# First two input blocks take the mLSTM keys' weights along; tokens held in quarter-feature tiles

## The chip, the cores and the metric

The kernel runs on one core of a Trainium2 chip. The metric is the time of one execution on that core in microseconds (us), taken as the median of several runs. The engines named below are TensorE (PE, with its weight loads as PEld), VectorE (DVE), ScalarE (ACT), GpSimd (POOL) and SyncE (SP), which here does little but issue DMAs.

## What is computed

Two transformer blocks in a row on 256 tokens of 2048 features, in float32. Only the beginning of the first one is touched. There, an input `x` (256 tokens) and a context `ctx` (256 tokens) are normalised, scaled and shifted by a modulation that is itself computed from `w_mod`, and multiplied with one wide weight matrix `w_in`:

```
mod   = c_act  @ w_mod + b_mod          # for x;   mod_c = cc_act @ w_mod + b_mod  for ctx
h     = rmsnorm(x,   g_norm1) * (1 + sc1)  + sh1
hc    = rmsnorm(ctx, g_norm1) * (1 + csc1) + csh1
z     = h @ w_in        # and hc @ w_in
gq, gk, gv, gg, glr, mq, mk, mv, mo, mgate = split(z)   # columns: gk at 512, gv at 1024,
                                                        # mq at 3088, mk (mLSTM keys) at 3600, mv at 4112
ml_k  = mk.reshape(heads) * DK ** -0.5
```

Everything after it (the gated linear attention and mLSTM scans, the output projection `w_out`, the feed-forward network, and the whole second block) is left as it is.

## The kernel before

Float32 operands are split in two: `split_w` lets ACT cast a raw weight unit to a high part `wh` (L187), and DVE subtract to get the low part `wl` (L188). A product then takes three matmuls (`mm3`, L208 to L210: high by high, high by low, low by high). A weight unit is 512 KB, 256 rows of 512 columns, one DMA by SP (`load_raw`, L172), and `units` gives them one after the other. The pools of `raw`, `wh` and `wl` have 4 buffers each. The pool `b8` has 14 buffers of 8 KB per partition; it holds the tokens, the transposed activations `hc` and `hl` (two parts each), the accumulators `gvc` and `gv`, and also the tiles `wm` of modulation weights that SP loads (L475). PSUM has four `acc` banks, three `ps` banks and one `mod` bank.

The inputs stage (`mix_in`) runs over 8 blocks of 256 features. For block b, `pieces(b)` multiplies the block's slice of `hl` and `hc` (four token tiles, `forms`) with three weight units: the GLA keys (columns 512 to 1023, summed over all blocks in the four `acc` banks), and the GLA values in two halves, whose part sums DVE adds into `gvc` and `gv` (L612 and L614). One piece is one token tile by one unit: 6 matmuls of 512 columns. Then come the 8 matmuls of the gates (L630). Between the pieces the next block is made ready: `mod_pe` for block b+1 in five steps, of which four load one `wm` tile (512 KB in two DMAs, L475) and multiply it (L481) and the last one evacuates the sum (ACT L486, PE transposes L488, DVE L490, L497, L499); and `hidden(b+1, 0)` and `hidden(b+1, 1)`, which transpose the tokens of x and of ctx (L305), scale and shift them (DVE L314, ACT L312) and split them (ACT L290, DVE L291). A block can't start on PE before that.

After the eight blocks comes the keys stage: `a_form` multiplies all 16 feature tiles with the mLSTM keys' weights (column 3600) in 8 units of 24 matmuls, and `k_evac` copies the four sums out of PSUM on ACT (L678) and transposes two of them (L684). Queries and values stages follow.

Two streams of side work hang on the main loops. Each unit that `units` yields calls `tick()`, which advances the stream `mods` (the remaining modulation vectors, `mod_vec`: each step loads one 512-KB tile of `w_mod`, L172, and DVE folds it in with two operations, L514 and L516) and the stream `side`. `mods` is set up at block 4 and runs at a rate of one step per unit there and in the keys stage. In `mix_out`, when the output projection has been written down, L1197 forces the steps that are still missing (`while self.mods_done < 12`).

The program is written in this order, and a scheduler then sets each engine's order by priority and by when operands are there; the two casts of a weight unit have a raised priority. In each engine the instructions run in that order.

The tokens are in four `b8` tiles, two halves of the features for x (`xt[2]`, `xt[3]`) and for ctx (`xt[0]`, `xt[1]`). A half is free again after the last of its four blocks has been transposed.

## Time and profile before

| | |
|---|---|
| median of 3 runs | 2670.62 us (2667.31 to 2674.35) |
| the profiled execution | 2672.57 us |
| its span in the trace | 2670.4 us |
| granted clock, mean | 0.991 of full speed |
| PE busy | 2603.5 us, 97% of the span |
| DVE busy | 1846.4 us, 69% |
| ACT busy | 1281.8 us, 48% |
| HBM read and written | 556.4 MB, 208 GB/s over the span |

2.2 us of the profiled execution lie outside its span. The times of the rows below count from the span's start. The inputs stage ends and the keys stage begins at some 240 us, the queries follow at some 300 us, and the forced steps of the modulation lie at 712 to 726 us.

### The profile page before, as it was taken

To read this page: it belongs to the slowest core of one execution; us is meant where nothing else is said; L and a number is where in the kernel's file an instruction comes from. 1 tells how busy PE (TensorE), PEld (TensorE's weight loads), DVE (VectorE), ACT (ScalarE), POOL (GpSimd) and SP (SyncE) were. 2 spreads that over 40 slices of the span, in tenths; PEclk is the share of its full clock that TensorE was granted. 3 is DMA by queue.
4 is the path that set the end of the run, shared out by engine and by line. 5 is a ranking of instruction groups with operands and counts; after the bars stand their busy time and mean duration, and the time that the engine had idled before them with its cause. 6 is when DMAs were issued, how large, how long until landed. Compare 5 with 4: busy or idle time off the path is not lost.

```text
span 2670.4 us, 37499 instructions
## 1 busy us (share of the span) xinstructions
PE 2603.5 (97%) x14093; PEld 2190.4 (82%) x14093; DVE 1846.4 (69%) x3006; ACT 1281.8 (48%) x2008; POOL 26.5 (1%) x52
## 2 busy tenths in 40 slices
PE   5999999999899999999999999999999999999999
PEld 3666888877778888888888988888888889998888
DVE  4466678787778988857856867677755566666665
ACT  2223323344365555544534554555544455657553
POOL 1000000000000000000000000000000000000000
PEclk8999999999999999999999999999999999999999
DMA  9775466678876666666675666556665567645664
GB/s 333 246 239 173 143 211 199 226 224 265 274 260 220 210 220 206 226 218 205 204 243 179 215 190 189 190 189 189 197 232 189 185 208 215 166 143 173 201 217 159
DMA packets 345271, 558.89 MB, mean 209 GB/s; under 512 B 30692, under 2 KB 129178, under 8 KB 342402
## 3 DMA queue, kind: packets, MB, share of 16 engines
q1 hardware_dynamic: 339800, 548.54, 63.9%
q10 hardware_dynamic: 4746, 7.11, 0.7%
q8 instruction: 110, 1.80, 0.3%
q0 software_dynamic: 544, 0.86, 0.1%
q14 instruction: 71, 0.58, 0.1%
HBM read 541.75 MB, written 14.69 MB: 208 GB/s over the span
## 4 chain that ended last, share of the span: by engine, by line
PE 82%; DMA 8%; DVE 6%; ACT 2%; issue 2%; SPq 1%; POOL 0%; ACTq 0%; DVEq 0%
PE acc L237 20%; PE acc L210 10%; PE acc L208 10%; PE acc L209 10%; PE acc L238 10%; PE mod L237 5%; DMA raw<-in_w_in_dram 3%; PE mod L238 2%; PE mod L209 2%; PE mod L210 2%; PE mod L208 2%; DMA raw<-in_w_mod_dram 2%; DVE wl L188 2%; DMA raw<-in_w_out_dram 1%; DVE ev L516 1%
## 5 line engine op out<-in xcount | busy, mean ns | idle before, releaser
L188 DVE TENSOR_TENSOR wl<-raw,wh 128x1024 fp32r<-128x1024 f32 (+4 forms) x804 | 965.7, 1205 | 578.2 <-ACT wh L187 575.5
L187 ACT CAST wh<-raw 128x1024 fp32r<-128x1024 f32 (+4 forms) x804 | 829.6, 1036 | 1068.0 <-PE acc L210 345.7
L237 PE MATMUL acc<-b,wh 128*128 128x512 f32 x2336 | 821.1, 394 | 0.0
L238 PE MATMUL acc<-b,wl 128*128 128x256 f32 x2336 | 634.4, 281 | 1.1 <-DVE wl L188 1.0
L208 PE MATMUL acc<-wh,b 128*128 128x512 f32 (+3 forms) x1580 | 585.3, 373 | 10.0 <-ACT b L290 7.6
L209 PE MATMUL acc<-wl,b 128*128 128x512 f32 (+3 forms) x1580 | 586.6, 371 | 7.5 <-DVE wl L188 7.3
L210 PE MATMUL acc<-wh,b 128*128 128x512 f32 (+3 forms) x1580 | 576.2, 370 | 1.1 <-DVE b L291 0.6
L237 PEld LDWEIGHTS acc<-b,wh 128*128 128x128 f32 x2336 | 434.1, 188 | 88.9 <-issue 0.7
L238 PEld LDWEIGHTS acc<-b,wl 128*128 128x128 f32 x2336 | 438.9, 188 | 15.0 <-DVE wl L188 2.4
L208 PEld LDWEIGHTS acc<-wh,b 128*128 128x128 f32 x1580 | 298.8, 189 | 71.8 <-ACT b L290 9.4
L209 PEld LDWEIGHTS acc<-wl,b 128*128 128x128 f32 x1580 | 299.2, 189 | 62.1 <-DVE wl L188 12.6
L210 PEld LDWEIGHTS acc<-wh,b 128*128 128x128 f32 x1580 | 297.0, 189 | 55.6 <-DVE b L319 4.0
L516 DVE SCALAR_TENSOR_TENSOR ev<-raw,cs,ev 128x512 f32<-128x512 f32 x240 | 179.4, 747 | 59.1 <-DMA raw<-in_w_mod_dram 56.4
L237 PE MATMUL mod<-b,wh 128*128 128x512 f32 x576 | 215.5, 396 | 0.6 <-DVE t L249 0.6
L238 PE MATMUL mod<-b,wl 128*128 128x256 f32 x576 | 161.5, 280 | 0.7 <-DVE wl L188 0.7
L237 PEld LDWEIGHTS mod<-b,wh 128*128 128x128 f32 x576 | 108.4, 188 | 23.5 <-DVE t L249 1.1
L1367 DVE SCALAR_TENSOR_TENSOR t<-t,convw,t 128x189 f32<-128x189 f32 (+2 forms) x344 | 126.9, 423 | 0.0
L238 PEld LDWEIGHTS mod<-b,wl 128*128 128x128 f32 x576 | 108.3, 188 | 3.9 <-DVE wl L188 1.1
L208 PE MATMUL mod<-wh,b 128*128 128x512 f32 (+2 forms) x274 | 96.9, 354 | 0.0
L209 PE MATMUL mod<-wl,b 128*128 128x512 f32 (+2 forms) x274 | 96.7, 353 | 0.0
L210 PE MATMUL mod<-wh,b 128*128 128x512 f32 (+2 forms) x274 | 96.5, 352 | 0.0
L290 ACT CAST b<-t 128x256 fp32r<-128x256 f32 x123 | 47.2, 405 | 64.2 <-DVE t L314 44.1
(357 smaller groups left out, 2469.0 us busy)
## 6 DMA issues: line engine op xcount, KB each, us to landing
raw<-in_w_up_dram SPq DMA_DIRECT2D x160, 512.0 KB, 4.5
raw<-in_w_mod_dram SPq DMA_DIRECT2D x128, 512.0 KB, 4.5
raw<-in_pool_w_in_dram SPq DMA_DIRECT2D x128, 512.0 KB, 3.8
raw<-in_w_in_dram SPq DMA_DIRECT2D x96, 512.0 KB, 4.9
raw<-in_w_down_dram SPq DMA_DIRECT2D x83, 512.0 KB, 4.8
b<-in_w_mod_dram SPq DMA_DIRECT2D x64, 512.0 KB, 7.9
raw<-in_pool_w_out_dram SPq DMA_DIRECT2D x64, 512.0 KB, 4.0
raw<-in_ple_w_gate_dram SPq DMA_DIRECT2D x64, 512.0 KB, 3.9
```

Source lines behind the costliest of these rows:

```text
L187: nc.scalar.copy(wh[:, :n], raw[:, :n])
L188: nc.vector.tensor_tensor(out=wl[:, :n], in0=raw[:, :n], in1=wh[:, :n].bitcast(F32), op=ALU.subtract)
L208: mm(out, lh, rh, start=first, stop=False)
L209: mm(out, lh, rl, start=False, stop=False)
L210: mm(out, ll, rh, start=False, stop=last)
L237: mm(acc, wh[:, i, o], f.both(kt), start=kt == k_first, stop=False)
L238: mm(acc[:, :T], wl[:, i, o], f(kt)[0], start=False, stop=kt == k_last)
L290: nc.scalar.copy(h, src)
L516: nc.vector.scalar_tensor_tensor(out=ev, in0=rv[:, i, :], scalar=cc, in1=ev, op0=ALU.mult, op1=ALU.add)
L1367: nc.vector.scalar_tensor_tensor(out=ov[:, r0:r1, c0:c1], in0=uv[:, r0 + dy:r1 + dy, c0 + dx:c1 + dx], scalar=tap(ky, kx), in1=ov[:, r0:r1 ...
```

## The change

The tokens go into four tiles that x and ctx share: tile q holds the features 512q to 512q+511 of both, and so belongs to the blocks 2q and 2q+1. Each input is loaded in four DMAs of 512 KB instead of two of 1 MB, and scaled by 8 DVE operations of 512 columns instead of 4 of 1024.

The blocks 0 and 1 (`early = 2`) load the mLSTM keys' weights of their rows as a fourth unit, multiply them in four more pieces each, and DVE puts the sums into a new `b8` tile `mk0`. The keys stage then runs over the remaining 6 units, and `k_evac` adds `mk0` on DVE while it evacuates, and scales on ACT afterwards.

```diff
     def tokens(self, i, src):
-        for half in range(2):
-            self.xt[i + half] = self.b8((P, 2, 1024))
-            self.nc.sync.dma_start(self.xt[i + half], src[0, :, half * 1024:(half + 1) * 1024].rearrange(
+        for q in range(4):
+            if self.xt[q] is None:
+                self.xt[q] = self.b8((P, 4, 512))
+            self.nc.sync.dma_start(self.xt[q][:, i:i + 2, :], src[0, :, q * 512:(q + 1) * 512].rearrange(
                 "(t p) n -> p t n", p=P))
...
-                for half, tt in ((0, 0), (0, 1), (1, 0), (1, 1)):
-                    t = self.xt[i + half][:, tt, :]
+                for q, tt in [(q, tt) for q in range(4) for tt in range(2)]:
+                    t = self.xt[q][:, i + tt, :]
                     nc.vector.tensor_scalar(out=t, in0=t, scalar1=r[:, tt:tt + 1], scalar2=None, op0=ALU.mult)
...
+        early = 2
+        mk0 = self.b8((P, 4, 512))
...
+            if b < early:
+                for tt in order:
+                    acc = self.ps()
+                    self.a_form([acc], [forms[tt]], ws[b, 3], kts[0], kts[-1])
+                    add(mk0[:, tt, :], acc)
+                    yield 1
...
-                ws[b, i] = list(self.units(w, 512 + 512 * i, 512, range(*blocks[b])))
+                ws[b, i] = list(self.units(w, 512 + 512 * i if i < 3 else 3600, 512, range(*blocks[b])))
...
         weights(0, 2)
+        weights(0, 3)
...
                     weights(b + 1, 2)
+                    if b + 1 < early:
+                        weights(b + 1, 3)
...
-                nc.scalar.activation(out=t, in_=accs[tt], func=AF.Copy, scale=scale)
+                if part is None:
+                    nc.scalar.activation(out=t, in_=accs[tt], func=AF.Copy, scale=scale)
+                else:
+                    nc.vector.tensor_tensor(out=t, in0=accs[tt], in1=part[:, tt, :], op=ALU.add)
+                    nc.scalar.mul(t, t, scale)
...
-        self.a_form(accs, forms, self.units(w, 3600, 512, range(16)), 0, 15)
-        self.mkc = k_evac(accs, self.mk, float(P) ** -0.5)
+        self.a_form(accs, forms, self.units(w, 3600, 512, range(2 * early, 16)), 2 * early, 15)
+        self.mkc = k_evac(accs, self.mk, float(P) ** -0.5, mk0)
```

PE at the end of block 0, before. The last piece of the values ends, then come the fourth `wm` tile of block 1's modulation (L481), the gates (L630), the transposes that evacuate the modulation (L488) and the first tile of block 2's modulation; `acc` with `wh_59` opens block 1.

```order
L209 MATMUL ps_87_424<-wl_57_257,b8_11_120 128x512
L210 MATMUL ps_87_424<-wh_56_256,b8_11_120 128x512
L481 MATMUL mod_61_272<-b8_71_342,cs_81 32x512 x4
L630 MATMUL ps_88_432<-b8_11_120,t4_53_246 112x256 x4
L630 MATMUL ps_88_432<-b8_15_124,t4_53_246 112x256 x4
L488 MATMUL mod_61_272<-cst_68,t2_72_349 128x128 x4
L481 MATMUL mod_92_454<-b8_93_455,cs_81 32x512 x4
L208 MATMUL acc_22_131<-wh_59_262,b8_15_124 128x512
L209 MATMUL acc_22_131<-wl_60_263,b8_15_124 128x512
L208 MATMUL acc_23_132<-wh_59_262,b8_15_124 128x512
L209 MATMUL acc_23_132<-wl_60_263,b8_15_124 128x512
```

The same place on PE in the changed kernel, from the end of the first added piece (`ps_95`); the fourth `wm` tile stands six matmuls ahead of these rows (lines of the file have moved by one here).

```order
L208 MATMUL ps_95_457<-wh_60_275,b8_17_132 128x512
L209 MATMUL ps_95_457<-wl_61_276,b8_17_132 128x512
L210 MATMUL ps_95_457<-wh_60_275,b8_17_132 128x512
L489 MATMUL mod_65_291<-cst_68,t2_76_368 128x128 x4
L208 MATMUL ps_96_465<-wh_60_275,b8_17_132 128x512
L209 MATMUL ps_96_465<-wl_61_276,b8_17_132 128x512
L210 MATMUL ps_96_465<-wh_60_275,b8_17_132 128x512
L208 MATMUL ps_96_465<-wh_60_275,b8_17_132 128x512
L209 MATMUL ps_96_465<-wl_61_276,b8_17_132 128x512
L210 MATMUL ps_96_465<-wh_60_275,b8_17_132 128x512
L208 MATMUL acc_24_139<-wh_63_281,b8_17_132 128x512
L209 MATMUL acc_24_139<-wl_64_282,b8_17_132 128x512
```

Between the modulation's last multiply and block 1 stand two of block 0's four added pieces, while the gates and block 2's first modulation tile have moved behind the opening of block 1.

DVE at the same place, before: the copies of block 0's last pieces (L612), the reduction of the modulation (L490), its vectors (L497, L499), and the scale and shift of block 1's tokens (L314), with the low parts of two weight units (L188) in between.

```order
L612 COPY b8_24_133<-ps_87_424 128x512
L612 COPY t2_19_128<-ps_88_432 112x512
L490 TENSOR_REDUCE sm_73_355<-mod_61_272 128x8
L188 TENSOR_TENSOR wl_78_379<-raw_76_376,wh_77_378 128x1024
L497 TENSOR_TENSOR mod0_97<-sm_73_355,vec1_87 128x4
L497 TENSOR_TENSOR mod1_98<-sm_73_355,vec1_87 128x4
L188 TENSOR_TENSOR wl_91_445<-raw_89_442,wh_90_444 128x1024
L499 TENSOR_TENSOR mod1_98<-mod1_98,vec1_87 128x4
L314 TENSOR_SCALAR t1_80_387<-ps_79_382,mod1_98,mod0_97 128x256
L314 TENSOR_SCALAR t1_85_416<-ps_84_411,mod1_98,mod0_97 128x256
L291 TENSOR_TENSOR b8_15_124<-t1_80_387,b8_15_124 128x256
```

DVE there in the changed kernel: L616 copies a piece, L491, L498 and L500 are the modulation, L314 the tokens.

```order
L616 COPY b8_27_142<-ps_94_449 128x512
L188 TENSOR_TENSOR wl_82_398<-raw_80_395,wh_81_397 128x1024
L616 COPY b8_26_141<-ps_95_457 128x512
L491 TENSOR_REDUCE sm_77_374<-mod_65_291 128x8
L498 TENSOR_TENSOR mod0_101<-sm_77_374,vec1_91 128x4
L498 TENSOR_TENSOR mod1_102<-sm_77_374,vec1_91 128x4
L500 TENSOR_TENSOR mod1_102<-mod1_102,vec1_91 128x4
L314 TENSOR_SCALAR t1_87_412<-ps_86_407,mod1_102,mod0_101 128x256
L314 TENSOR_SCALAR t1_92_441<-ps_91_436,mod1_102,mod0_101 128x256
L616 COPY b8_26_141<-ps_96_465 128x512
L291 TENSOR_TENSOR b8_17_132<-t1_87_412,b8_17_132 128x256
```

The weight units no longer stand between the modulation and L314; a copy of the added pieces stands ahead of the modulation, and one behind L314.

DVE at the first block's context tokens, before: `t1_46` is the transposed context, L447 casts the masks, L291 makes the low part.

```order
L188 TENSOR_TENSOR wl_57_257<-raw_55_254,wh_56_256 128x1024
L188 TENSOR_TENSOR wl_60_263<-raw_58_260,wh_59_262 128x1024
L291 TENSOR_TENSOR t4_53_246<-t4_52_239,t4_53_246 128x8x48
L291 TENSOR_TENSOR t4_54_247<-t4_52_239,t4_54_247 128x8x48
L314 TENSOR_SCALAR t1_46_222<-ps_45_217,mod1_98,mod0_97 128x256
L447 CAST lev_988<-t4_182_989 128x896
L291 TENSOR_TENSOR b8_11_120<-t1_46_222,b8_11_120 128x256
```

In the changed kernel L314 stands ahead of the second L188 and the L291 of this low part ahead of the masks' cast (L448):

```order
L188 TENSOR_TENSOR wl_58_270<-raw_56_267,wh_57_269 128x1024
L314 TENSOR_SCALAR t1_47_235<-ps_46_230,mod1_102,mod0_101 128x256
L188 TENSOR_TENSOR wl_61_276<-raw_59_273,wh_60_275 128x1024
L291 TENSOR_TENSOR t4_54_259<-t4_53_252,t4_54_259 128x8x48
L291 TENSOR_TENSOR t4_55_260<-t4_53_252,t4_55_260 128x8x48
L291 TENSOR_TENSOR b8_13_128<-t1_47_235,b8_13_128 128x256
L616 COPY b8_28_143<-ps_68_324 128x512
L616 COPY b8_28_143<-ps_73_345 128x512
L448 CAST lev_1077<-t4_197_1078 128x896
L291 TENSOR_TENSOR b8_13_128<-t1_48_239,b8_13_128 128x256
```

What moved there is the masks' cast, from one place ahead of the L291 to three places behind it.

SP at the end of the output projection (`w_out`), before: five units of `w_mod` after the last unit of `w_out`, of those that L1197 forces.

```order
L172 DMA raw_1005_5548<-in_w_mod_dram 128x2x512
L172 DMA raw_1006_5552<-in_w_out_dram 128x4x256
L172 DMA raw_1011_5593<-in_w_mod_dram 128x2x512
L172 DMA raw_1012_5597<-in_w_mod_dram 128x2x512
L1183 DMA t2_992_5450<-gtd_1024 128x256
L172 DMA raw_1013_5601<-in_w_mod_dram 128x2x512
L172 DMA raw_1014_5605<-in_w_mod_dram 128x2x512
L172 DMA raw_1015_5609<-in_w_mod_dram 128x2x512
L172 DMA raw_1018_5621<-in_w_mod_dram 128x2x512
```

SP there in the changed kernel:

```order
L172 DMA raw_1012_5573<-in_w_mod_dram 128x2x512
L172 DMA raw_1013_5577<-in_w_out_dram 128x4x256
L172 DMA raw_1018_5618<-in_w_mod_dram 128x2x512
L172 DMA raw_1019_5622<-in_w_mod_dram 128x2x512
L1200 DMA t2_997_5467<-gtd_1113 128x256
L172 DMA raw_1020_5626<-in_w_mod_dram 128x2x512
L172 DMA raw_1021_5630<-in_w_mod_dram 128x2x512
L172 DMA raw_1022_5634<-in_w_mod_dram 128x2x512
L172 DMA raw_1023_5638<-in_w_mod_dram 128x2x512
L172 DMA raw_1024_5642<-in_w_mod_dram 128x2x512
L172 DMA raw_1027_5654<-in_w_mod_dram 128x2x512
```

Two more units of `w_mod` come after the last one of `w_out`, seven in place of five.

## Rows read from the trace of the kernel before

**Rows 1.** The page's first part: the span, and busy time of each engine.

```profile
span 2670.4 us, 37499 instructions
PE 2603.5 (97%) x14093; PEld 2190.4 (82%) x14093; DVE 1846.4 (69%) x3006; ACT 1281.8 (48%) x2008; POOL 26.5 (1%) x52
```

**Rows 2.** Stretches: engines' busy us (instructions), PEclk granted clock, DMA share, GB/s.

```profile
40.00:60.00 20.00, 17.07 (x84) 10.98 (x88) 8.96 (x16) 2.32 (x4) 2.52 (x5) 0.91 1.09 361
60.00:80.00 20.00, 17.12 (x81) 10.64 (x73) 7.46 (x16) 5.75 (x10) 0.00 (x0) 0.83 0.73 249
200.00:220.00 20.00, 16.94 (x85) 11.09 (x84) 14.64 (x29) 5.14 (x9) 0.00 (x0) 1.00 0.91 291
260.00:280.00 20.00, 20.00 (x77) 14.13 (x76) 11.09 (x20) 9.38 (x12) 0.00 (x0) 1.00 0.26 79
```

**Rows 3.** PE's timeline, block 0 to 1: start, duration, instruction, [idle before <- releaser].

```profile
35.91 0.30 PE L305 MATMUL ps<-cst,b 128*128 128x128 f32 x1 [1.22 <-issue]
...
42.36 0.79 PE L208 MATMUL acc<-wh,b 128*128 128x512 f32 x1 [3.02 <-ACT b L290]
...
45.85 0.73 PE L210 MATMUL acc<-wh,b 128*128 128x512 f32 x2 [0.57 <-DVE b L291]
...
54.17 0.40 PE L209 MATMUL ps<-wl,b 128*128 128x512 f32 x1
...
56.49 0.40 PE L210 MATMUL ps<-wh,b 128*128 128x512 f32 x1
...
62.85 1.06 PE L481 MATMUL mod<-b,cs 128*32 128x512 f32 x8 [0.44 <-DVE sm L490]
66.35 0.80 PE L208 MATMUL acc<-wh,b 128*128 128x512 f32 x1 [2.44 <-ACT b L290]
66.94 0.63 PE L209 MATMUL acc<-wl,b 128*128 128x512 f32 x1
...
69.50 0.63 PE L209 MATMUL ps<-wl,b 128*128 128x512 f32 x1
...
71.64 0.63 PE L208 MATMUL acc<-wh,b 128*128 128x512 f32 x1
```

**Rows 4.** DVE's timeline at the same place.

```profile
59.89 0.69 DVE L612 COPY b<-ps 128x512 f32<-128x512 f32 x1 [2.28 <-PE ps L210]
...
62.71 1.22 DVE L188 TENSOR_TENSOR wl<-raw,wh 128x1024 fp32r<-128x1024 f32 x1
...
63.99 1.22 DVE L188 TENSOR_TENSOR wl<-raw,wh 128x1024 fp32r<-128x1024 f32 x1
...
65.32 1.00 DVE L314 TENSOR_SCALAR t<-ps,mod,mod 128x256 f32<-128x256 f32 x2
```

**Rows 5.** PE's timeline: modulation multiplies in block 4 (first two rows) and block 6.

```profile
144.83 1.07 PE L481 MATMUL mod<-b,cs 128*32 128x512 f32 x8
...
149.20 1.06 PE L481 MATMUL mod<-b,cs 128*32 128x512 f32 x8
...
201.29 1.06 PE L481 MATMUL mod<-b,cs 128*32 128x512 f32 x8 [0.30 <-DMA b<-in_w_mod_dram]
```

**Rows 6.** SP's timeline: DMA issues around the same two places.

```profile
129.79 4.85 SPq L475 DMA_DIRECT2D b<-in_w_mod_dram  x4
...
180.35 0.38 SPq L172 DMA_DIRECT2D raw<-in_w_in_dram  x1
195.82 2.02 SPq L475 DMA_DIRECT2D b<-in_w_mod_dram  x4
```

**Rows 7.** DVE's timeline in the forced steps of the modulation.

```profile
720.05 1.54 DVE L516 SCALAR_TENSOR_TENSOR ev<-raw,cs,ev 128x512 f32<-128x512 f32 x2 [0.36 <-DMA raw<-in_w_mod_dram]
722.13 1.54 DVE L516 SCALAR_TENSOR_TENSOR ev<-raw,cs,ev 128x512 f32<-128x512 f32 x2 [0.55 <-DMA raw<-in_w_mod_dram]
```

**Rows 8.** PE's timeline at the end of the forced steps.

```profile
725.81 1.84 PE L543 MATMUL ps<-cst,ev 128*128 128x2 f32 x8 [4.41 <-DVE ev L516]
```

**Rows 9.** Waits, 232 to 320 us: total, times, longest us.

```profile
ACT t L678 <- PE acc L210: 2.3, 3, 0.8
```

**Rows 10.** The page's DMA issues: times, KB each, median us to landing.

```profile
b<-in_w_mod_dram SPq DMA_DIRECT2D x64, 512.0 KB, 7.9
```

8 lines of the change are left out of this document (4 added, 4 removed).

## The prediction, made before the changed kernel was run

> **What bounds the kernel now.** I read the page's totals first: PE is busy for 97% of the span, DVE for 69% [rows 1]. So time is to be had only where PE stands still or where its clock is low, and moving work from a full stage into a hole is worth just what the hole holds. The table of stretches shows where holes are: in 40 to 80 us PE has about 17 busy us of 20, at a granted clock of 0.91 and 0.83, and in 260 to 280 us, the keys stage, it has all 20 at 1.00 [rows 2]. Next I read PE's timeline through the first hole, for the idle times in brackets and their releasers. Between block 0 and block 1 it waits 0.44 us for DVE's reduction and 2.44 us for the cast of block 1's tokens [rows 3]. Ahead of block 0's context half it waits 3.02 us for such a cast, and then 0.57 us for a DVE subtract [rows 3]. From the same rows come the two prices of a matmul: from 54.17 to 56.49 us ten starts pass, 0.232 us each; from 66.94 to 69.50 us six starts pass, 0.427 us each, which is the lower of the two levels, 1.2 GHz, right after the idle time. The twelve matmuls from 66.35 to 71.64 us took 5.29 us where 2.78 would have done at the higher level: 2.5 us lost [rows 3]. Then I followed the two wait chains that the change touches elsewhere: the modulation tiles of the inputs stage, on SP and PE [rows 5, 6], and the forced modulation steps at 720 us, on DVE and PE [rows 7, 8].
>
> **The change part by part.** *The work that moves.* Two blocks with four pieces of six matmuls are 48 matmuls; at 0.232 us they add 11.1 us to the inputs stage and take 11.1 us from the keys stage, where PE has no idle time [rows 2]. So −11.1 is sure there, as long as the 6 units left come in time (the DMA share there is 0.26 [rows 2]).
>
> *What of it is free in the inputs stage.* In the changed order two added pieces, 12 matmuls and 2.8 us, stand between the last modulation multiply of block 0 and the first matmul of block 1, where PE waited 0.44 + 2.44 = 2.9 us [rows 3]. The chain behind that wait also becomes shorter: DVE no longer makes two low parts between the modulation and L314; they took 62.71 to 63.84 and 63.99 to some 65.1 us, 1.22 us each by duration [rows 4]. In their place stands one copy of a piece, 0.69 us by the nearest row [rows 4]. I therefore take 2.8 us of the 11.1 as hidden; the bounds are 0, if the pieces only push the wait back, and 2.9, if all of it goes. The other 36 matmuls stand in a dense row and are paid. The DVE copies and adds, eight of 0.69 us, fall on an engine that had 2.28 us idle before such a copy [rows 4]; without that cover, the three `ps` banks would hold PE up by at most 0.69 us each time.
>
> *The clock.* With 2.9 us of idle time gone, I expect the lower level after it to go too: −2.5 us. Bounds 0 and −2.5. The nearest row for a short idle is the one of 1.22 us at 35.91 us, after which starts are at the full rate; the nearest for a long one is that of 2.44 us itself [rows 3]. The idle left is about 0.6 us, nearer to the first.
>
> *The start.* DVE now takes the squares of the quarter context tiles in between the steps of the first block's modulation, and they wait for the tiles. By the order, the first matmul comes some 2.1 us later, of which the 1.22 us idle at 35.91 us takes up most: +0.9. The context's L314 passes one low part (1.22 us), which shortens the 3.02 us wait; its L291 no longer stands behind the masks' cast, which frees the 0.57 us [rows 3, 4]. Together 0.9 − 1.2 − 0.6 = −0.9, bounds +2.1 (nothing taken up) and −3.6 (both waits gone). The eight scalings of 512 columns in place of four of 1024 go with the rest of DVE's work here. Two more weight units of 512 KB at 361 GB/s [rows 2] are 1.45 us each of a saturated DMA stretch, put on SP's queue ahead of modulation tiles; none of the waits of PE in that stretch is for a DMA [rows 3], so I take 0 with bounds 0 and +1.5.
>
> Inputs stage: 11.1 − 2.8 − 2.5 − 0.9 = +4.9. With the keys stage: −6.2 us.
>
> *What is given back.* First, the modulation tiles. `mk0` takes one of the 14 `b8` buffers for the whole stage. By the addresses in the built program, the fourth tile of block 5's modulation then lands in the buffer of the first one of the same block; in the old one its buffer was free long before, and SP issued it at 129.79 us with three others [rows 6]. The first tile is multiplied at 144.83 us for 1.07 us, the fourth is wanted at 149.20 us [rows 5]. The like case is in block 6: SP, held from 180.35 us, issued at 195.82 us, and PE took the tile at 201.29 us after 0.30 us of waiting for it [rows 5, 6], 5.4 us after the issue. So 145.9 + 0.1 + 5.4 − 149.2 = +2.2 us of PE idle. Queued behind on SP are the next `w_mod` and `w_in` units. Bounds: 0, if the planner's order on the chip leaves more room, and +4.7, if the lower clock level follows with its 2.5 us.
>
> Second, the forced steps. The two ticks that went from the keys stage into blocks 0 and 1, where no stream is set, leave the modulation two steps behind, and SP's order has seven `w_mod` units in place of five after the last `w_out` unit. A step is two DVE operations, 1.54 us, and the units arrive just behind them (0.36 and 0.55 us of waiting) [rows 7]; at the end of that chain PE had stood for 4.41 us [rows 8]. So 2 × 1.54 = +3.1 us. Bounds: 0, if DVE's earlier idle time takes the steps up, and +4.2 with two more such DMA waits.
>
> Third, `k_evac`. An add from PSUM and an ACT pass over the tile replace one ACT pass that PE did not wait for: ACT itself waited 2.3 us in three turns for PE's sums [rows 9]. The transposes of the keys now come directly behind the last matmuls in PE's order. One add, by the nearest row, is 0.69 us [rows 4], and the ACT pass about the same again; I take +1.0, between 0 and 2.5.
>
> Sum: −6.2 + 2.2 + 3.1 + 1.0 = +0.1 us on the profiled execution's 2672.6 us. That execution lies 2.0 us above the median of the three runs, and the difference carries over to the median: 2670.6 + 0.1, or 2671 us. I call anything within 0.3% (8 us), about what a measurement of this kernel can tell from no change, the same.
>
> **A rule that speaks against the change.** In rows: the loads in 40 to 60 us are of 512 KB, like the new token loads [rows 10], and they moved 361 GB/s at a DMA share of 1.09 [rows 2], so a load of 512 KB costs no rate when others are in flight. The Trainium skill, "DMA: Bandwidth & Descriptors", section "Bandwidth", asks for loads of at least 1 MiB, and its fit of about 2.0 us plus bytes over 436 GB/s (made on the GpSimd path) would give an estimated 8 × 3.2 us for the tokens where the old loads had 4 × 4.4 us, some 8 us more if they ran one after the other. By that the sum would be +8 us; this trace disagrees, with its 361 GB/s.
>
> **The rivals.** (A) *Nothing is given back.* The planner placed these steps with estimated durations, and DVE may take up the two steps, since it waits for tiles before them; then −6.2 stands: 2664.4 us, and with the bound of the start 2661.7. For it: DVE is 69% busy [rows 1]. Against it: the row of 4.41 us shows that those steps end late already [rows 8].
> (B) *Slower: the held modulation tile.* In block 4, SP stands in front of the fourth tile, and what is queued behind comes late as well. The same hold in block 6 left PE 16.94 busy us of 20 in 200 to 220 us [rows 2], 3.1 us lost. With the lower clock level the price is 2.2 + 2.5 + 3.1 = 7.8 in place of 2.2, and the sum +5.7: 2676.3 us. It decides from a price of 2.1 on (slower than before) and passes 8 us only from 10.1 on. Against it: the next `w_in` unit behind that tile has many microseconds until its block starts.
> (C) *The change doesn't do what it says: the hole moves.* The two pieces run, but block 1's tokens wait just as long behind them, and the clock falls as before: +2.8 + 2.5, sum +5.4, 2676.0 us. Against it: the shortened DVE chain [rows 4].
> (D) *The smaller token loads cost.* Four more issues by SP at the start (x and ctx, two more each) at 0.38 us [rows 6] that nothing hides: +1.5, 2672.2 us.
>
> **How the numbers follow.** My forecast (a gain of 6 us at the front given back in three places) 0.39, with its own range of ±4 us; A 0.30; B 0.16; C 0.11; D 0.04. The predicted time is the forecast's, 2671 us. The range leaves out the best tenth and the worst tenth: down to 2661, A with the start's bound; up to 2680, B or C with one further bound, such as the +3.0 us from the start's −0.9 to its bound of +2.1. A goes beyond −8 us where the start gains as well, which I give half of its cases; with 0.05 from the forecast, should two of its three give-backs and the start come out better, that makes faster 0.20. B and C pass +8 in under half of their cases, 0.12. The rest, 0.68, is within 0.3%.
>
> **What would show it.** In the changed trace: PE's wait before block 1 falls from 2.9 to under 1 us and starts are at 0.23 us after it (right for the clock term); the keys stage loses 48 matmuls and 11 us; a wait for a DMA of `w_mod` of about 2 us on PE in block 4, near 150 us; the wait for L516 before the small matmuls that evacuate those steps (L543 before) rises from 4.4 to some 7 us; a wait of about 1 us at the keys' transposes. If the last three are missing, A is right. If the wait before block 1 is still there, C. If a wait in block 4 is longer than 4 us and is followed by starts at 0.43 us, B. If the first matmul comes more than 3 us later and nothing behind takes it up, my term for the start is wrong, and D is to be looked at.

## The result, and the profile after

| | before | changed |
|---|---|---|
| median | 2668.97 us (2665.8 to 2674.35, 4 runs) | 2687.22 us (2684.19 to 2689.16, 4 runs) |
| ratio, 95% interval | | 1.0067 [1.0054, 1.0081] |
| span of the profiled execution | 2670.4 us | 2687.4 us |

The changed kernel is slower, by 18 us; 2671 us had been forecast, with 2680 us as the upper end. One execution of a later experiment (e12, 3654.07 us) was in a slow state and counts in no ratio below. The changed kernel's page begins:

```profile
span 2687.4 us, 37538 instructions
PE 2616.2 (97%) x14093; PEld 2194.0 (82%) x14093; DVE 1857.5 (69%) x3026; ACT 1281.7 (48%) x2007; POOL 26.4 (1%) x52
```

The number of matmuls is the same and PE is still busy for 97%, but its busy time has grown by 12.7 us [rows 1]: the same matmuls took longer. In part that is the clock, whose mean is 0.987 in this execution and 0.991 in that of before. It is not the whole: another of the four executions had 0.991 as well and took 2688.83 us. The totals don't tell where the time goes. The table of stretches does [rows 2] (busy us of PE, PEld, DVE, ACT, POOL, then granted clock, DMA share, GB/s):

```profile
40.00:60.00 20.00, 19.65 (x102) 12.11 (x103) 12.48 (x23) 4.19 (x6) 2.53 (x5) 1.00 1.08 361
60.00:80.00 20.00, 20.00 (x102) 12.62 (x101) 9.26 (x15) 4.92 (x9) 0.00 (x0) 1.00 1.08 371
...
260.00:280.00 20.00, 20.00 (x70) 13.60 (x69) 8.52 (x18) 9.74 (x14) 0.00 (x0) 0.91 0.00 0
...
380.00:400.00 20.00, 15.95 (x73) 12.33 (x73) 13.42 (x19) 5.75 (x6) 0.00 (x0) 0.83 0.17 55
...
620.00:640.00 20.00, 14.69 (x65) 11.08 (x64) 15.41 (x26) 9.87 (x18) 0.00 (x0) 0.83 0.76 250
...
720.00:740.00 20.00, 9.69 (x83) 9.49 (x81) 16.26 (x31) 3.49 (x10) 1.19 (x1) 0.82 0.81 272
```

The last three stretches before the change:

```profile
380.00:400.00 20.00, 19.46 (x96) 15.79 (x95) 16.61 (x21) 7.00 (x8) 0.00 (x0) 1.00 0.85 267
...
620.00:640.00 20.00, 20.00 (x91) 16.12 (x90) 15.78 (x23) 10.28 (x16) 0.00 (x0) 1.00 0.82 267
...
720.00:740.00 20.00, 13.17 (x60) 10.50 (x59) 14.42 (x28) 8.83 (x18) 0.70 (x1) 0.83 0.96 344
```

The hole between 40 and 80 us is gone, clock included, as forecast. Two new ones stand at 380 to 400 and at 620 to 640 us, where the clock is lower too, and the one at 720 to 740 us has grown. PE's timeline between block 0 and 1 answers [rows 3]; the wait before block 1 (2.44 us, then starts at 0.427 us) has become 0.35 us, and block 1 opens at 60.77 us instead of 66.35 us, at the full rate:

```profile
39.84 0.50 PE L208 MATMUL acc<-wh,b 128*128 128x512 f32 x1 [0.19 <-ACT b L290]
...
59.18 0.50 PE L208 MATMUL ps<-wh,b 128*128 128x512 f32 x1 [0.35 <-DVE b L616]
...
60.77 0.50 PE L208 MATMUL acc<-wh,b 128*128 128x512 f32 x1
61.10 0.40 PE L209 MATMUL acc<-wl,b 128*128 128x512 f32 x1
61.34 0.40 PE L208 MATMUL acc<-wh,b 128*128 128x512 f32 x1
```

So at 61 us the changed kernel is 5.6 us ahead, and has done two added pieces besides. Where does it lose that and 17 us more? PE's waits, longest first, in three stretches (300 to 420, 600 to 660, 700 to 760 us; total, times, longest) name three places:

```profile
PE ps L1022 <- DVE b L1015: 4.1, 1, 4.1
...
PE acc L208 <- ACT b L322: 5.2, 1, 5.2
...
PE ps L544 <- DVE ev L517: 11.2, 1, 11.2
```

Before the change the last wait was 4.41 us [rows 8], the second was missing, and the first was

```profile
PE ps L1005 <- DVE b L998: 1.4, 1, 1.4
```

L1022 are the score matmuls of the gated linear attention, `side` work that runs between the weight units of the values stage; L322 casts the transposed input of the output projection `w_out`; L544 closes the forced modulation steps. Set against the same matmuls of the kernel before, unit by unit, the changed kernel is 8.9 us late at the end of the inputs stage, 2.9 us early at 320 us, 8.2 us late at 388 us, 2.8 us late at the last unit of `w_in` and 12.2 us late at the first of `w_out`. These are single profiles. Where one and the same kernel was profiled twice (e11 and e16 below), the two lie up to 8 us apart in such a comparison, though their spans differ by 4.4 us; in 310 to 320 us, for one, the granted clock was 1.00 in e11 and 0.52 in e16, with PE busy throughout. A few us between two profiles are therefore no finding by themselves.

### The profile page after: what moved, and what is told of

Its sections match the earlier page's. It is cut to its first block, busy times and chain, and to the rows that moved or that the text cites. A ratio compares the mean times of both kernels' runs of the same rounds, so it can differ in the third digit from the quotient of the medians.

```text
span 2687.4 us, 37538 instructions
## 1 busy us (share of the span) xinstructions
PE 2616.2 (97%) x14093; PEld 2194.0 (82%) x14093; DVE 1857.5 (69%) x3026; ACT 1281.7 (48%) x2007; POOL 26.4 (1%) x52
## 4 chain that ended last, share of the span: by engine, by line
PE 82%; DMA 8%; DVE 5%; ACT 2%; issue 2%; SPq 1%; POOL 0%; ACTq 0%; DVEq 0%
PE acc L237 19%; PE acc L210 10%; PE acc L208 10%; PE acc L209 10%; PE acc L238 10%; PE mod L237 5%; DMA raw<-in_w_in_dram 3%; DMA raw<-in_w_mod_dram 3%; PE mod L238 2%; PE mod L209 2%; PE mod L208 2%; PE mod L210 2%; DVE wl L188 1%; DVE ev L517 1%; PE ps L208 1%
## 5 line engine op out<-in xcount | busy, mean ns | idle before, releaser
L188 DVE TENSOR_TENSOR wl<-raw,wh 128x1024 fp32r<-128x1024 f32 (+4 forms) x804 | 966.4, 1205 | 580.6 <-ACT wh L187 575.9
L237 PE MATMUL acc<-b,wh 128*128 128x512 f32 x2336 | 823.9, 395 | 0.0
L238 PE MATMUL acc<-b,wl 128*128 128x256 f32 x2336 | 636.4, 282 | 0.1
L208 PE MATMUL acc<-wh,b 128*128 128x512 f32 (+3 forms) x1564 | 577.3, 372 | 11.0 <-ACT b L322 5.2
L209 PE MATMUL acc<-wl,b 128*128 128x512 f32 (+3 forms) x1564 | 579.8, 371 | 4.2 <-DVE wl L188 3.9
L210 PE MATMUL acc<-wh,b 128*128 128x512 f32 (+3 forms) x1564 | 571.4, 371 | 0.7 <-DVE b L319 0.3
L237 PEld LDWEIGHTS acc<-b,wh 128*128 128x128 f32 x2336 | 434.1, 188 | 90.5 <-issue 0.7
L238 PEld LDWEIGHTS acc<-b,wl 128*128 128x128 f32 x2336 | 439.3, 188 | 13.5 <-DVE wl L188 0.8
L208 PEld LDWEIGHTS acc<-wh,b 128*128 128x128 f32 x1564 | 295.7, 189 | 71.0 <-issue 7.0
L210 PEld LDWEIGHTS acc<-wh,b 128*128 128x128 f32 x1564 | 293.6, 189 | 58.0 <-DVE b L319 4.0
L517 DVE SCALAR_TENSOR_TENSOR ev<-raw,cs,ev 128x512 f32<-128x512 f32 x240 | 179.5, 748 | 68.4 <-DMA raw<-in_w_mod_dram 66.1
L237 PE MATMUL mod<-b,wh 128*128 128x512 f32 x576 | 215.7, 396 | 0.6 <-DVE t L249 0.6
L238 PE MATMUL mod<-b,wl 128*128 128x256 f32 x576 | 161.8, 281 | 0.7 <-DVE wl L188 0.7
L237 PEld LDWEIGHTS mod<-b,wh 128*128 128x128 f32 x576 | 108.2, 188 | 23.8 <-DVE t L249 1.1
L238 PEld LDWEIGHTS mod<-b,wl 128*128 128x128 f32 x576 | 108.4, 188 | 3.9 <-DVE wl L188 1.1
```

Of the source, the lines that this page charges most:

```text
L188: nc.vector.tensor_tensor(out=wl[:, :n], in0=raw[:, :n], in1=wh[:, :n].bitcast(F32), op=ALU.subtract)
L208: mm(out, lh, rh, start=first, stop=False)
L209: mm(out, lh, rl, start=False, stop=False)
L210: mm(out, ll, rh, start=False, stop=last)
L237: mm(acc, wh[:, i, o], f.both(kt), start=kt == k_first, stop=False)
L238: mm(acc[:, :T], wl[:, i, o], f(kt)[0], start=False, stop=kt == k_last)
```

## The experiments

Theory T at the start: the two lost ticks, which put the side streams behind, make most of the loss, at places far from the change. Rival S: the held buffer and the new tiles, in the inputs stage. Rival R: any change shuffles the scheduler's order, with gains and losses at other places. All times are medians; ratios are to the kernel before, run on the same chip.

| run | what | median us | ratio, 95% interval |
|---|---|---|---|
| e1 | changed, both ticks back | 2668.52 | 0.9997 [0.9987, 1.0007] |
| e2 | before, two ticks less | 2683.63 | 1.0061 [1.0043, 1.0079] |
| e3 | quarter tiles alone | 2664.03 | 0.9977 [0.9968, 0.9987] |
| e4 | early keys alone, half tiles | 2709.18 | 1.0151 [1.0135, 1.0166] |
| e5 | changed, modulation's ticks back | 2665.86 | 0.9988 [0.9979, 0.9997] |
| e6 | changed, side stream's ticks back | 2693.50 | 1.0090 [1.0069, 1.0110] |
| e7 | quarter tiles, modulation at 1.25 | 2681.00 | 1.0045 [1.0030, 1.0061] |
| e8 | quarter tiles, one buffer held | 2668.17 | 0.9991 [0.9982, 0.9999] |
| e9 | changed, two steps put in at the values | 2673.49 | 1.0015 [1.0004, 1.0026] |
| e10 | changed, two steps put in at `w_out` | 2682.71 | 1.0055 [1.0038, 1.0072] |
| e11 | quarter tiles, early in block 0, tick back | 2662.37 | 0.9971 [0.9958, 0.9983] |
| e12 | quarter tiles, output rate 0.625 | 2675.95 | 1.0018 [1.0006, 1.0030] |
| e13 | changed, evacuation by the mod bank | 2672.14 | 1.0017 [1.0007, 1.0027] |
| e14 | e7, evacuation by the mod bank | 2655.26 | 0.9955 [0.9937, 0.9972] |
| e15 | before, evacuation by the mod bank | 2667.80 | 0.9997 [0.9985, 1.0008] |
| e17 | changed with both repairs of e14 | 2662.43 | 0.9968 [0.9955, 0.9980] |
| e18 | the same, early in block 0 alone | 2671.29 | 1.0007 [0.9998, 1.0017] |

**Which part costs (e1 to e4).** e1 changes the keys stage:

```diff
+        def paced():
+            for i, u in enumerate(self.units(w, 3600, 512, range(2 * early, 16))):
+                if i < early:
+                    self.tick()
+                yield u
-        self.a_form(accs, forms, self.units(w, 3600, 512, range(2 * early, 16)), 2 * early, 15)
+        self.a_form(accs, forms, paced(), 2 * early, 15)
```

> The changed kernel, but the keys stage ticks the two streams of side work twice at each of its first two units, so that the two ticks lost with the moved units are given back (SP's order then has five w_mod units after the last w_out unit again, as before the change). Theory T (the two lost ticks put the modulation and the side work two steps behind, and that costs behind the keys stage: forced steps, start of the output projection): some 10 us faster than the changed kernel, about 2677 us, PE's wait for the forced steps back from 11.3 to some 4.5 us. Rival S (buffers: mk0 and the new token tiles cost in the inputs stage): only the forced steps gain, 3 us at most, about 2684. Rival R (any change of the program makes the scheduler put the work in another order, with gains and losses at other places): the wait of the forced steps falls, but other waits of several us appear elsewhere, total not foreseeable within 2670 to 2690.

e2 does the reverse to the kernel before:

```diff
+        def quiet():
+            tick, self.tick = self.tick, lambda: None
+            for i, u in enumerate(self.units(w, 3600, 512, range(16))):
+                if i == 1:
+                    self.tick = tick
+                yield u
-        self.a_form(accs, forms, self.units(w, 3600, 512, range(16)), 0, 15)
+        self.a_form(accs, forms, quiet(), 0, 15)
```

> The kernel before the change, with nothing moved, but the first two units of the keys stage don't tick: the streams of side work are two steps behind, as in the changed kernel. Theory T: most of the loss is here, some 10 us slower than before, about 2679 us, with a wait of some 8 to 11 us at the forced steps. Rival S: 2669 to 2673, the two steps cost 0 to 3 us. Rival R: anything from 2665 to 2685, with waits that differ from those of the changed kernel.

e3 and e4 take the change apart:

```diff
-        early = 2
-        mk0 = self.b8((P, 4, 512))
+        early = 0
+        mk0 = None
...
-        weights(0, 3)
```

> Only the token tiles of the change: quarter-feature tiles shared by x and ctx, no early keys, no mk0. Theory T: as before within 3 us, about 2669. Rival S: 3 to 8 us slower, by waits in the first 250 us. Rival R: differs from before by several us at places behind 250 us, though nothing there was changed.

e4 has the old `tokens` and `normalise`, with the new `early`, `mk0`, fourth units and `k_evac`:

```diff
+        early = 2
+        mk0 = self.b8((P, 4, 512))
...
+            if b < early:
+                for tt in order:
+                    acc = self.ps()
+                    self.a_form([acc], [forms[tt]], ws[b, 3], kts[0], kts[-1])
+                    add(mk0[:, tt, :], acc)
+                    yield 1
```

> The other part of the change alone: early keys of two blocks with mk0, but the tokens in half-feature tiles as before. Theory T: the loss is that of the changed kernel, about 2687 us, as the ticks are lost here too. Rival S: slower still, 2690 or more, since mk0 takes a buffer and the tokens free none before block 4. Rival R: between 2670 and 2690, with other waits.

The ticks are it. Giving them back takes away all 18 us, more than the 10 us I had expected; taking them from the old kernel, where nothing else is changed, costs 14.6 us. PE's waits of e2 in the same three stretches stand at the same places as those of the changed kernel:

```profile
PE ps L1011 <- DVE b L1004: 4.6, 1, 4.6
...
PE acc L208 <- ACT b L322: 6.7, 1, 6.7
...
PE ps L543 <- DVE ev L516: 9.6, 1, 9.6
```

and in e1 the first falls to 1.4 us, the second is missing, and the third reads

```profile
PE ps L544 <- DVE ev L517: 5.2, 1, 5.2
```

Quarter tiles alone gain 5 us, which I had not forecast; early keys in half tiles lose 40 us, for which the lost ticks (14.6 us) don't suffice, so there rival S has its part.

Both parts close the wait between block 0 and block 1 (0.44 + 2.44 us before) by themselves. This is PE's last wait ahead of block 1 in e3, without any added piece, and in e4, with half tiles:

```profile
61.37 0.50 PE L208 MATMUL acc<-wh,b 128*128 128x512 f32 x1 [0.60 <-ACT b L290]
```
```profile
64.07 0.50 PE L208 MATMUL ps<-wh,b 128*128 128x512 f32 x1 [0.35 <-DVE b L615]
```

In e3 the clock is 1.00 in 40 to 80 us as well. So in the changed kernel, with both parts, the two added pieces had only these 0.60 us left to fill.

**The held buffer (e8).** On the quarter tiles of e3:

```diff
+        held = self.b8((P, 4, 512))
+        nc.gpsimd.memset(held[:, 0, 0:2], 0.0)
...
+        nc.gpsimd.tensor_copy(self.sm([P, 2]), held[:, 0, 0:2])
```

> Quarter token tiles without early keys, but one buffer of the b8 pool is held from the start of the inputs stage to the end of the keys stage by a tile that GpSimd writes and reads two columns of; no work is moved. If the held buffer is what makes the inputs stage grow by more than the moved work (16.7 us instead of 11.1 between quarter tiles alone and the changed kernel): the inputs stage ends some 5 us later than with quarter tiles alone, and the time is some 5 us longer, about 2669. If it is the order or the added DVE work: no difference, 2664.

The first keys transpose marks the end of the inputs stage. In PE's timelines it stands, for the kernel before, the changed one, e3, e8 and e4, at:

```profile
240.08 0.60 PE L684 MATMUL ps<-cst,t 128*128 128x128 f32 x4
```
```profile
248.97 0.60 PE L701 MATMUL ps<-cst,t 128*128 128x128 f32 x4
```
```profile
232.31 0.60 PE L700 MATMUL ps<-cst,t 128*128 128x128 f32 x4
```
```profile
239.35 0.60 PE L702 MATMUL ps<-cst,t 128*128 128x128 f32 x4
```
```profile
267.61 0.49 PE L700 MATMUL ps<-cst,t 128*128 128x128 f32 x3
```

Quarter tiles bring the end 7.8 us forward, and one held buffer takes 7.0 us of it. The 11.1 us of moved work then sum up to 240.1 − 7.8 + 7.0 + 11.1 = 250.4 us, measured 249.0, so 1.4 us of the moved work would be hidden. That is within what profiles of one and the same inputs stage differ by: this matmul lies at 236.5 to 240.1 us in three profiles with the old stage (before, e2, e15), at 232.3 to 234.0 us in four with quarter tiles alone (e3, e7, e12, e14), and at 247.7 to 250.9 us in the eight with quarter tiles and two early blocks. Against those four, the one profile of e8 puts the held buffer's price at 5.4 to 7.0 us. With half tiles the stage ends 27.5 us later than before, 16.4 us more than the moved work. PE waits there (e4, 80 to 270 us) for modulation tiles for 8.4 us in all, 5.6 us the longest, which speaks for the buffer; a held buffer by itself was not tried with half tiles.

**Which stream (e5, e6), and when (e9, e10).** In `paced`, e5 has `self.mods.tick()` and e6 `self.side.tick()` in place of `self.tick()`; e9 and e10 call `self.mods.step()` twice, at the start of the values stage and of `mix_out`.

> The changed kernel with the two lost ticks given back to the modulation stream alone; the side stream stays two steps short in the keys stage. If the modulation's lag is what costs (theory M): as with both ticks back, about 2669 us, and the forced steps' wait back to some 4.5 us. If the side stream's lag costs as well (theory N): the forced steps recover, but 5 us or more stay, 2675 to 2682.

> The changed kernel with the two lost ticks given back to the side stream (the GLA context state) alone; the modulation stays two steps behind. Theory M: nothing gained, 2684 to 2688, with the waits at some 386 us, at the start of the output projection and at the forced steps still there. Theory N: 2672 to 2680, with the wait at some 386 us gone and that of the forced steps still at some 11 us.

> The changed kernel, with the modulation's two missing steps put in together at the start of the values stage, some 320 us, ahead of everything that lost time in the changed kernel. If the lag of the modulation stream behind the side work of the values stage is what costs at 385 us, at the start of the output projection and at the forced steps: as with the ticks back in the keys stage, 2664 to 2670. If it is enough that the order of the keys and queries stages was another one: nothing gained, 2680 or more.

> The changed kernel, with the modulation's two missing steps put in at the start of the output projection. The forced steps are five again, so their wait should come back from 11.3 to some 4.5 us, but the wait of 4.1 us at 385 us stays. If the start of the output projection (the 9 us by which it came later than its last input unit) hangs on the lag too, it stays or grows: 2676 to 2684 in all. If the three losses are independent: 2680.

It is the modulation stream alone: with its ticks 2665.86 us, with those of the other 2693.50 us (above the 2684 to 2688 us expected, though its interval overlaps that of the changed kernel). Put in at the values stage, ahead of the first loss, the steps bring back 14 of 18 us, short of the 2664 to 2670 us expected. At `w_out` they shorten the wait at the forced steps to 5.1 us, but the other two waits stay (4.1 and 5.3 us); the median is 4.5 us lower, which is not clear of noise, since the two intervals overlap.

**Is it lateness (e7, e12)?** Both are quarter tiles without early keys:

```diff
-MODS = {"inputs": 1.0, "keys": 1.0, "values": 1.25, "gates": 0.75, "output": 0.5, "ffn": 0.15}
+MODS = {"inputs": 1.0, "keys": 1.25, "values": 1.25, "gates": 0.75, "output": 0.5, "ffn": 0.15}
```

> Quarter token tiles without early keys, and the modulation stream at 1.25 steps per unit in the keys stage in place of 1.0 (two steps ahead instead of two behind; SP's order has two forced w_mod units after the last w_out unit). Theory T (the phase of the modulation stream sets the forced steps' wait, 11.3 us at seven units, some 4.5 at five): 3 us or more faster than quarter tiles alone (2664), about 2660, and a wait under 2 us there. Rival R (only the scheduler's order is shuffled): 2660 to 2680 with waits elsewhere.

and e12 has 0.625 for the output instead.

> Quarter tiles without early keys, and the modulation stream at 0.625 instead of 0.5 steps per unit in the output projection, which leaves everything ahead of it in its order; the forced steps fall from five to about one or two. Theory T: the wait of some 4.5 us at the forced steps falls to under 2 us, and the time to some 2661. Rival R: another order in the output projection costs as much, 2664 or more.

Here theory T fell in the form I had given it, and rival R came out: another order, with waits elsewhere. Two steps ahead costs 17 us against e3, much as two steps behind costs 14.6 us against the old kernel. PE's waits in e7, 300 to 420 us, and in the forced steps:

```profile
PE ps L1021 <- DVE b L1014: 7.6, 1, 7.6
...
PE acc L208 <- ACT t L322: 7.1, 1, 7.1
```

The wait for the forced steps is gone there, and a wait of 7.1 us for the normalised tokens behind them, which those steps may have hidden before, takes its place. e12 shows the same (1.5 us, then 8.2 us) and loses 12 us against e3. What counts is not being late but *at which unit* the steps fall. PE's order, row numbers first (tile names without their middle number), tells why at the score matmuls; two rows are one group. Before the change these are the first two score groups, the evacuation of a modulation vector (L523), and the third score group:

```
1123 L1005 MATMUL ps_2553   1124 L1005 MATMUL ps_2559
1189 L1005 MATMUL ps_2610   1190 L1005 MATMUL ps_2616
1199 L523  MATMUL ps_2697
1249 L1005 MATMUL ps_2704   1250 L1005 MATMUL ps_2710
```

In the changed kernel, the third and fourth group, the evacuation (L524) and the fifth group:

```
1253 L1022 MATMUL ps_2722   1254 L1022 MATMUL ps_2728
1270 L1022 MATMUL ps_2775   1271 L1022 MATMUL ps_2781
1272 L524  MATMUL ps_2821
1317 L1022 MATMUL ps_2840   1318 L1022 MATMUL ps_2846
```

Between two groups lies a chain over DVE and ACT, whose last link is an operation of 2.29 us on DVE (L1015). In the changed kernel's trace, the chain and the groups around it on DVE and PE:

```profile
383.14 2.48 DVE L1009 TENSOR_TENSOR b<-b 128x512 f32<-128x512 f32 x4
387.68 2.29 DVE L1015 TENSOR_TENSOR b<-b,b 128x2048 f32<-128x2048 f32 x1 [2.06 <-ACT b L1013]
```
```profile
380.53 1.95 PE L1022 MATMUL ps<-b 128*128 128x128 f32 x16
...
390.02 3.78 PE L1022 MATMUL ps<-b 128*128 128x128 f32 x16 [4.05 <-DVE b L1015]
```

From 383.14 to 389.97 us the chain takes 6.8 us. With 64 rows of projection in between, some 15 us at 0.23 us each, PE has work meanwhile; with 15 rows it waits 4.1 us. The wait is not the whole price: the clock is 0.83 in 380 to 400 us, and the group behind the wait takes 3.78 us instead of 1.95. In e7 three groups follow each other, with nothing but an evacuation between the first two and nothing at all between the second and the third; ahead of the third PE waits 7.6 us. The rows between the first four groups are 64, 58 and 63 before the change and in e3, 64, 59 and 65 in e5, but 70, 59 and 15 in the changed kernel and 71, 59 and 14 in e2. The groups and the evacuation (`ps_2697`, `ps_2821`) take turns at the same three `ps` banks, so the next test takes the evacuation off them.

**The banks (e13 to e15).** Once the inputs stage is over, the mod bank has no user until the feed-forward network, so the evacuations can go there (`psm`):

```diff
-            pt = self.ps()
+            pt = self.psm() if hasattr(self, "queries") and not self.five else self.ps()
...
-        pv = self.ps()[:, :8].rearrange("p (k r) -> p k r", r=2)
+        pv = (self.psm() if hasattr(self, "queries") and not self.five else self.ps())[:, :8].rearrange("p (k r) -> p k r", r=2)
```

e13 does so in the changed kernel, e14 in e7, e15 in the kernel before.

> The changed kernel, with nothing given back, but from the keys stage to the output projection the modulation stream evacuates its vectors through the mod bank of PSUM, which stands free there, instead of one of the three ps banks that the GLA score groups (L1022) and the transposes of the output stage (L305) use as well. Theory P (an evacuation that comes at another unit shifts the turns of the ps banks, so that score groups and transposes land close behind each other in PE's order): the wait of 4.1 us of L1022 at 385 us is gone and the values stage keeps its lead, the forced steps' wait of 11 us stays: 2674 to 2680. Rival Q (the lag costs by DVE's work and not by banks): the wait stays, 2684 to 2690.

> Quarter tiles without early keys, the modulation at 1.25 steps per unit in the keys stage (that was 2681, with PE standing 7.7 us between two score groups), evacuations through the mod bank as in the last one. Theory P: no two score groups directly behind each other, the 7.7 us gone, and the forced steps short as well: 2662 to 2668. Rival Q: 2676 or more.

> The kernel before the change, only with the evacuations through the mod bank. Theory P: the order was already good there, so little is gained, 2664 to 2674. If the mod bank alone gains 5 us or more here, what e13 and e14 gain isn't the repair of an unlucky order but a gain of its own.

In time the control e15 shows no change (0.9997), e13 gains 15 us on the changed kernel, more than expected, e14 26 us on e7, also more than expected. The only wait of PE that the view lists from 300 to 420 us in e13 is

```profile
PE ps L991 <- ACT b L722: 0.9, 1, 0.9
```

and the groups are apart again. The evacuation now runs ahead of the third group, where it stood directly behind the fourth, and the fourth group follows 61 rows behind the third:

```profile
372.42 1.02 PE L524 MATMUL mod<-ev,cst 128*1 128x512 f32 x2
373.70 1.95 PE L1022 MATMUL ps<-b 128*128 128x128 f32 x16
...
389.60 1.95 PE L1022 MATMUL ps<-b 128*128 128x128 f32 x16
```

So the shared banks have their part in the score groups' wait: with the lag left as it was and the evacuation off these banks, it is gone. My reading is that the evacuation had to keep its turn behind the fourth group and drew that group forward; how the scheduler came to its order was not followed. At the start of `w_out` e13 still waits:

```profile
PE acc L208 <- ACT b L322: 5.8, 1, 5.8
```

There the mod bank cures nothing; what puts these transposes late stays open. At the forced steps the wait of 11 us, which I had expected to stay, is down to 0.4 us, but another stands there instead:

```profile
PE ps L305 <- DVE t L1250: 10.5, 2, 8.9
```

Nor is e15 as still as its time says. These are the stretches behind the score groups, before the change and in e15:

```profile
400.00:600.00 200.00, 192.04 (x965) 158.24 (x965) 156.62 (x276) 84.14 (x139) 8.53 (x12) 1.00 0.68 217
600.00:640.00 40.00, 40.00 (x194) 32.73 (x193) 32.04 (x49) 20.24 (x32) 0.00 (x0) 1.00 0.84 272
```
```profile
400.00:600.00 200.00, 199.98 (x1014) 166.99 (x1014) 160.90 (x282) 89.71 (x143) 9.01 (x12) 1.00 0.71 228
600.00:640.00 40.00, 30.44 (x138) 24.19 (x137) 27.48 (x40) 18.13 (x30) 0.00 (x0) 0.91 0.77 245
```

The mod bank takes 8 us of idle time out of the first stretch and puts 9.6 us into the second, with a wait of 8.1 us for L322 at the start of `w_out`, on a kernel whose modulation doesn't lag. So it has a gain of its own, which the old kernel loses again. For e13 this changes little: PE's wait at the score groups lies ahead of these stretches, and at 400 us its profile is some 14 us ahead of that of the changed kernel already. Of e14's 26 us it may be a part: PE stood for 17.0 us from 400 to 600 us in e7 and for 3.2 us in e14, and how much of that is the repaired order was not separated.

e14 is the fastest kernel of all, 2655.26 us, 14 us below the one before; its steps come early, its longest wait at a score group is 1.6 us, and no wait for L517 is left. The 7.2 us for ACT L322 at the forced steps stand in it as in e7.

**The early keys by themselves (e11, e16 to e18).** e11 is e5 with `early = 1`; e16, whatever its label says, runs the kernel of e11 again, once: 2667.3 us, 0.9 us outside what was expected. e17 has the changed kernel's two blocks, the mod bank and `"keys": 1.67` (ten steps in six units, as many as in e14), e18 `early = 1` and `"keys": 1.43`.

> Quarter tiles, early keys in block 0 alone (24 matmuls moved instead of 48), and the lost tick of the modulation stream given back. The held buffer is the same as with two blocks, the wait between block 0 and 1 is filled the same way. If the held buffer and not the moved work decides: about as with two blocks and the modulation's ticks (2666), within 2 us. If work moved into block 1 is paid for (no hole there) and only given back later: also 2666. If block 1's part gains by itself: 2668 or more here.

> A second look at quarter tiles with early keys in block 0 alone and the modulation's tick given back (2662.4 in the first run): within 4 us of that, and the inputs stage again ends some 4 us later than before the change.

> The changed kernel in full (quarter tiles, early keys in blocks 0 and 1) with both repairs of e14: evacuations through the mod bank, and 1.67 modulation steps per unit in the keys stage, which makes ten steps in six units as in e14. What is left against e14 (2655.3) is the price of the early keys alone. If they gain what their filled wait between blocks 0 and 1 suggests: 2650 to 2655. If the held buffer (7.1 us later at the end of the inputs stage) outweighs it: 2658 to 2664.

> The same with early keys in block 0 alone, and 1.43 steps per unit (ten steps in seven units). The held buffer costs the same as with two blocks, and the wait between blocks 0 and 1 is filled the same: as e17 within 2 us, if only these two count; better than e17 by 3 us or more, if the work in block 1 isn't hidden and its later tiles are held up as well.

e17 against e14 is the price of the early keys when the rest is repaired: 7.2 us in the medians. At 323 us e17 already is 7.6 us behind e14. So they lose, and by about what the held buffer costs; that it is the buffer is not shown, since at the end of the inputs stage e17 is behind by 3.7 us more than the moved work (248.78 against 233.96 us), and the rest arises behind it. One block (e11) is 3.5 us faster than two (e5), more than I had expected, though the second run, 4.9 us higher, makes this weak. e18 is a miss: 9 us slower than e17 where I had expected it equal or better. It was 2.9 us ahead of e17 at 323 us and lost that lead only at the start of `w_out` and behind it, so some order there may be unlucky again; I did not follow it.

## Why the prediction was wrong, point by point

- **The wait between block 0 and 1, and the clock:** right in what happened. 2.9 us became 0.35, starts behind it are at 0.23 us, and the clock is 1.00 in 40 to 80 us. But I gave it to the added pieces alone, and the quarter tiles do it without them (0.60 us and the same clock in e3). So of the 2.8 us that I took as hidden work at most some 0.6 us were to be had, and what the quarter tiles gain in this stage beyond its start was no term of my sum.
- **The start:** first matmul 1.0 us later (30.24 instead of 29.21 us), the 3.02 us wait of the context half down to 0.19, so that this half opens at 39.84 instead of 42.36 us. The term of −0.9 was in its bounds and too small: −2.5 us.
- **The held buffer:** the place was right and the size wrong. The fourth modulation tile of block 5 is late as I worked out, 2.10 us where I had 2.2, and the clock fell behind it (0.83 in 150 to 160 us). The tile here is 1 MB, two issues of 512 KB [rows 10], not 512 KB as the description above has it, so four issues are two tiles:

```profile
155.27 1.34 PE L482 MATMUL mod<-b,cs 128*32 128x512 f32 x8 [2.10 <-DMA b<-in_w_mod_dram]
```
```profile
134.21 16.57 SPq L476 DMA_DIRECT2D b<-in_w_mod_dram  x4
```

  SP spent 16.57 us on those four issues. But the buffer's whole price in the stage is 5.4 to 7.0 us (e8, where PE waits 3.54 us for that tile), and I had 2.2 with 4.7 as a bound. The inputs stage grew by 8.9 us instead of 4.9.
- **The keys stage:** right, as far as single profiles tell. From 8.9 us late to 2.9 us early is 11.8 us, where 11.1 had been forecast. That the two agree so closely is in part luck: in its profile e10, whose program changes only at `mix_out`, goes from 10.8 us late to 4.0 us early, 14.8 us, and e1, with the ticks back, from 10.2 to 0.8 us late, 9.4 us.
- **`k_evac`:** no wait of PE at the keys' transposes shows in the timeline; +1.0 was too much.
- **The forced steps:** the term was mis-sized, +6.8 instead of +3.1 us. I priced a step by its two DVE operations and took the other steps to begin as early as before. In the changed kernel the DVE operations of all seven stand behind the last units of `w_out`; the first begin at 727.94 us, 1.5 us before PE's last matmul there:

```profile
727.94 5.48 DVE L517 SCALAR_TENSOR_TENSOR ev<-raw,cs,ev 128x512 f32<-128x512 f32 x7
```

- **The step that failed:** I followed the lost ticks to one place, the forced steps. I had read that the modulation would be two steps behind from the keys stage on, and costed only where the lag ends. What lies between went unexamined: each vector's evacuation now falls at another unit, with it the score groups stand elsewhere in PE's order, and the output's transposes come late. That is +8.4 us at 385 us and +9.4 us at the start of `w_out`, against which the range held nothing. Some 5 us of the first is regained by the last unit of `w_in` (from 8.2 us late to 2.8 us), so these losses don't simply add up to the 18 us. The order of both programs would have shown the first: 63 rows between the third and the fourth score group there, 15 here. Why the start of `w_out` comes late stays open.
- **The rivals:** A (nothing given back) did not happen; with the ticks given back, e1 and e5 take 2669 and 2666 us, between A and the forecast. B named a slower case, but put it at the tile in block 4, whose wait was what I had forecast. The row that it leans on, 16.94 busy us of 20 in 200 to 220 us, was read wrongly: before the change PE waits there 0.30 us for the tile, and 0.5, 0.8 and 1.1 us for DVE's sums (L614). C (the hole moves) is refuted by the 0.35 us. D may have a part in the start: the first matmul comes at 30.25 us with quarter tiles alone (e3) and at 29.07 us with half tiles and early keys (e4). The rule of the Trainium skill, "DMA: Bandwidth & Descriptors", section "Bandwidth", on loads of at least 1 MiB is not borne out here: the quarter tiles alone, with their 512-KB loads, are 5 us faster (e3). The size of the loads was not changed by itself.

## What to carry to other kernels

When work is moved from one loop to another, count what else hangs on the loop's turns: a side stream that is paced by them shifts by as many steps, and all that it shares (here three PSUM banks) is handed out in another order hundreds of microseconds later. Look for two links of a serial chain that end up close together in the tensor engine's order, and try a bank of its own for the side stream before tuning its pace: here that took 15 and 26 us off two kernels, and nothing off a third, where it moved the waits to another place. A gain forecast for one part of a change may already be had from another part; run each part alone. A tile that is kept through a stage costs a buffer in each load of that stage; measure that price by holding an empty buffer.

## What was not expected of the hardware

The feed-forward stage's matmuls, the same in number and order of size, run a little longer, taken together, in every other profile than in the one of before (1455.5 us). The page's group of L237 and L238, before:

```profile
L237 PE MATMUL acc<-b,wh 128*128 128x512 f32 x2336 | 821.1, 394 | 0.0
L238 PE MATMUL acc<-b,wl 128*128 128x256 f32 x2336 | 634.4, 281 | 1.1 <-DVE wl L188 1.0
```

and in e14:

```profile
L237 PE MATMUL acc<-b,wh 128*128 128x512 f32 x2336 | 824.4, 395 | 0.3 <-ACT wh L187 0.2
L238 PE MATMUL acc<-b,wl 128*128 128x256 f32 x2336 | 637.4, 282 | 0.9 <-DVE wl L188 0.8
```

That is 6.3 us over 4672 matmuls without a wait to name; in the changed kernel it is 4.8 us. The one kernel that was profiled twice, e11 and e16, has 1456.6 us both times, 1.1 us more than before, which speaks for the program and not for the run; what in the program does it was not tried.
